# A hybrid SSD and delta-rule layer: TensorE's instructions kept in the order of the text, one gate moved to an earlier scan, scan steps put in another order

## The chip, the cores and the metric

The kernel runs on one core of one Trainium2 chip. The metric is device time in microseconds (us): the median of the kernel before is 2363.67 us over 3 runs (2360.88 to 2366.65). Engines are called PE (TensorE matmuls; PEld is its weight loads), DVE (VectorE), ACT (ScalarE), POOL (GpSimd) and SP (SyncE, which issues the DMAs).

## The reference

One transformer-like layer over 320 kept tokens (a prompt with meta tokens ahead of it, and a batch of one sampled stretch), model width 2048, everything in float32. Cut to what matters:

```python
u = _rmsnorm(x, norm_mix_w)
z_a, xbc_a, dt_a, qkv_b, z_b, beta_b, a_b, gate_a, gate_b = split(u @ w_in)
xbc, conv_a_new = _causal_conv(xbc_a, conv_a, ssd_conv_w, ssd_conv_b)   # then silu; xs, bm, cm
ya, ssm_a_new = _ssd_scan(xs, softplus(dt_a + bias), -exp(ssd_a_log), bm, cm, h0)  # 4 groups of 8 heads
ya = _rmsnorm((ya + xs * ssd_d) * silu(z_a), ssd_norm_w)
qkv, conv_b_new = _causal_conv(qkv_b, conv_b, gdn_conv_w)               # then silu, l2norm of q and k
# in _gdn_scan, for each block of tokens, 4 groups of 4 heads:
lmat = where(strict, beta * (k @ k.T) * decay, 0)
tinv = triangular_solve(eye + lmat, eye)
u = tinv @ (v * beta); w = tinv @ (k * beta * exp(gcum)); wv = u - w @ s
o = (q * exp(gcum)) @ s + (q @ k.T * decay) @ wv
ob = _rmsnorm(ob, gdn_norm_w) * silu(z_b)
h = x + sigmoid(gate_a) * (ya @ w_out[:2048]) + sigmoid(gate_b) * (ob @ w_out[2048:])
h = h + square(relu(_rmsnorm(h, norm_mlp_w) @ w_up)) @ w_down
```

The result is `_rmsnorm(h, norm_f_w)` and the new convolution and scan states.

## The kernel before

**The big products.** Every product with a weight is made by `block()` as matmuls into `pbig`. A chunk of weights of 512 x 256 comes by a DMA of SP into `raw` (`wload`, L195, three buffers), ACT rounds it to `hi` (L61), DVE makes the rest `lo` (L64), three buffers each, and PE multiplies three times for each of eight (j, k): hi by the high part of the tokens, hi by their low part, lo by the high part. So a chunk is 24 `pbig` matmuls of 320 to 336 columns. The chunks stand in one list, `stream`, in the order of use, and `block` loads three ahead. In the start `uh` and `ul` are the two parts of the normed tokens, made piece by piece (16 pieces) from `ut`; in the output projections `yh` and `yl` take their place.

**Main and side.** `run(main, side)` writes two generators in turn: `main` yields after three matmuls of `pbig` what they should take (3 x 325 / 2400 = 0.41 us for 320 columns), `side` yields what main work should pass before its next step. Beside the scan of one group stand the output projection of the group before and the projections of the group after. Four SSD scans (`scan_ssd`) come first, then four delta-rule scans (`scan_gdn`, here scan 0 to 3), then the MLP. Beside scan 0 stand `out_a(3)` and the projection for scan 1; beside scan 1 the first merge gate `gate_a`, `out_b(0)` and the projection for scan 2. The delta-rule projection has convolutions, `c` on DVE; `gate_a` has products `sgt`.

**What sets the order.** After the text is written, a scheduler puts the instructions of every engine in an order of its own, within the dependencies; the first stretch (up to `manual.close()`) already keeps the text's order. So in this kernel the yields propose an order and the scheduler decides it, on PE also.

**The start.** Rows `prow`, `cra`, `sra`, `crb`, `srb` are loaded and turned into columns by PE (`pcol`, L84), DVE copies them to `cwa`, `sta`, `cwb`, `stb`. `dvec` (L485) is loaded by pieces of 4 bytes, then four small `pb` (L487 to L490), then `wt` (L500, L501). ACT makes `nega` from `pb` and `wtr` from `wt`, and PE multiplies it into `ptok`. In `tokens()` that becomes `la`, and PE its running sums `pcum`.

**The SSD scan.** For each of three blocks of tokens PE makes `pcb` and the turned `pxt`; ACT and DVE make `xw` and its two parts `xwr`, which PE needs for the states `ph`; `em` and `xt` are needed for `pyd`, the sum of squares `sq` for `prs`.

**The delta-rule scan.** For each of three blocks PE makes `pk`, `pkk`, `pqk` and `pq` (the last one turns q); `a` goes to memory and comes back as blocks of 32 x 32 in `ab`. Then DVE alone solves all blocks, 31 steps of a product `pr` and a sum `ubt` (L847, L848). ACT copies the result to `ub`, DMAs write it (`uD`, `uTD`) and read it back as `u` and `tr` (L860, L866). Then come two rounds (32, then 64): PE `pz<-tr,a`, ACT `z<-pz`, in the first round PE `ptr<-z,u`, and PE `pu<-u,z`. For each block of tokens follow `pv`, `pw`, `po`, `pS`, and on DVE the norm `so`, `on`, which PE turns in `pot`. The yields between `pq` and `pz` are

```python
yield 1.0                      # after the last pq
yield 4.8                      # after the loads of ab
yield 0.5 + 0.0028 * w * m     # after each of the 31 steps
yield 9.6                      # after the loads of u and tr
```

where `w * m` sums to 7512 over the 31 steps, so the 31 yields are 36.5 us together and all of them 51.9 us.

Of the kernel before, what the change touches and what calls it, by code (L numbers as in the profile page):

```python
# [8 lines left out]
F32 = mybir.dt.float32  # L9
F32R = mybir.dt.float32r  # L10
AF = mybir.ActivationFunctionType
ALU = mybir.AluOpType
AX = mybir.AxisListType

P = 128
# [27 lines left out]
def tile_hybrid_step(ctx: ExitStack, tc: tile.TileContext, i: dict, o: dict):  # L43
# [16 lines left out]
    def act(out, in_, func=AF.Copy, **kw):  # L60
        nc.scalar.activation(out=out, in_=in_, func=func, **kw)  # L61
# [6 lines left out]

    V, G = nc.vector, nc.gpsimd
    MUL, ADD, SUB = ALU.mult, ALU.add, ALU.subtract  # L70


    ident = const.tile([P, P], F32, name="ident")
# [71 lines left out]
    def plan_proj(c0):  # L145
        plan([(0, win[:, c0:c0 + 256])], KD)

    def plan_out(r0):
        for b in range(8):
            plan([(0, wout[r0:r0 + 512, b * 256:(b + 1) * 256])], 4)  # L150
# [8 lines left out]
    def plan_gdn(g):  # L159
        for c0 in (C_K, C_Q, C_V, C_ZB):  # L160
            for b in range(2):
                plan_proj(c0 + g * 512 + b * 256)
# [7 lines left out]
    plan_out(1024)  # L170
    plan_gdn(0)
    plan_out(1536)
    plan_gdn(1)
    for b in range(8):
        plan_proj(C_GA + b * 256)
    plan_out(2048)
    plan_gdn(2)
    plan_out(2560)
# [334 lines left out]
    def tokens():  # L513

        yield 1.0
        for c in range(3):
            lo, n = CH_LO[c], CH_N[c]
            ps = scr("ptk")
            transp(ps[:n, :P], tokT[:, lo:lo + n])
            V.tensor_copy(tok[:n, c, :], ps[:n, :64])  # L520
            tt(V, tok[:n, c, :], tok[:n, c, :], ps[:n, 64:P], ADD)


        nega = sp.tile([P, 48], F32, name="nega")
        act(nega, pb[:, 1, :], AF.Exp)
        V.tensor_scalar(out=nega, in0=nega, scalar1=-1.0, scalar2=None, op0=MUL)
        sx = sp.tile([P, 3, 48], F32, name="sx")
        for a, b, t0 in ((0, 32, 0), (32, 48, 48)):
            tt(V, sx[:, :, a:b], tok[:, :, t0:t0 + b - a], pb[:, 0:1, a:b].to_broadcast([P, 3, b - a]), ADD)
        e = sp.tile([P, 3, 48], F32, name="e")  # L530
        s_ = sp.tile([P, 3, 48], F32, name="s_")
        s2 = sp.tile([P, 3, 48], F32, name="s2")
        pl = sp.tile([P, 3, 48], F32, name="pl")
        stt(e, sx, -1.0, sx, MUL, ALU.max)
        act(e, e, AF.Exp, scale=-1.0)
        V.tensor_scalar(out=s_, in0=e, scalar1=2.0, scalar2=None, op0=ADD)
        V.reciprocal(s_, s_)
        tt(V, s_, s_, e, MUL)
        tt(V, s2, s_, s_, MUL)
        V.tensor_scalar(out=pl, in0=s2, scalar1=1.0 / 17, scalar2=None, op0=MUL)  # L540
        for d in (15, 13, 11, 9, 7, 5, 3):
            stt(pl, pl, 1.0 / d, s2, ADD, MUL)
        stt(pl, pl, 1.0, s_, ADD, MUL)
        V.tensor_scalar(out=pl, in0=pl, scalar1=2.0, scalar2=None, op0=MUL)
        stt(pl, sx, 0.0, pl, ALU.max, ADD)
        V.tensor_copy(dt, pl[:, :, 0:32])
        la = sp.tile([P, 3, 48], F32, name="la")
        tt(V, la, pl, nega.unsqueeze(1).to_broadcast([P, 3, 48]), MUL)
        act(beta, tok[:, :, 32:48], AF.Exp, scale=-1.0)
        V.tensor_scalar(out=beta, in0=beta, scalar1=1.0, scalar2=None, op0=ADD)  # L550
        V.reciprocal(beta, beta)

        yield 13.5
        pcum = scr("pcum")
        ptot = scr("ptot")
        pv = pcum[:, :144].rearrange("p (c h) -> p c h", h=48)
        tv = ptot[:, :288].rearrange("p (c h) -> p c h", h=48)
        mm(pv[:80, 0, :], tri[:80, :80], la[:80, 0, :])
        mm(pv[:, 1, :], tri, la[:, 1, :])
        mm(pv[:, 2, :], trib, la[:, 2, :])  # L560
        mm(tv[:, 0, :], ones[:80, :], la[:80, 0, :])
        mm(tv[:, 1, :], ones, la[:, 1, :])
        mm(tv[:, 2, :], blk, la[:, 2, :])
        mm(tv[:, 3, :], halfm[:, 0, :], la[:, 2, :])
        mm(tv[:, 4, :], halfm[:, 1, :], la[:, 2, :])
        V.tensor_copy(acs[:80, 0, :], pv[:80, 0, :])
        V.tensor_copy(acs[:, 1:3, :], pv[:, 1:3, :])
        tt(V, wdec, tv[:, 0:3, :], acs, SUB)
        act(wdec, wdec, AF.Exp)
        act(etot[:, 0, :], tv[:, 1, :], AF.Exp)  # L570
        act(etot[:, 1:3, :], tv[:, 3:5, :], AF.Exp)
        act(neg_eg, acs[:, :, 32:48], AF.Exp)
        V.tensor_scalar(out=neg_eg, in0=neg_eg, scalar1=-1.0, scalar2=None, op0=MUL)
        tt(V, wd, dt, wdec[:, :, 0:32], MUL)
        yield 2.5
        rows = sp.tile([48, 2, NT], F32, name="rows")
        prow_ = scr("prow")
        for c in range(3):
            lo, n = CH_LO[c], CH_N[c]
            transp(prow_[:48, lo:lo + n], acs[:n, c, :])  # L580
        V.tensor_copy(rows[:, 0, :], prow_[:48, :NT])
        act(rows[:, 1, :], prow_[:48, :NT], AF.Exp)
        nc.scalar.dma_start(rowd.rearrange("a h t -> h a t"), rows)

        yield 1.0
# [19 lines left out]
    def scan_ssd(g, sg, x4, bc, z4):  # L605
# [12 lines left out]
        sti = sg.tile([P, 4, P], F32, tag="sio", name="sio", bufs=2)  # L618
        nc.sync.dma_start(sti, i["state_ssd"][0, 0, gh].rearrange("(t h) p n -> (h p) t n", h=2))
        load_decay(0)  # L620
        yield 4.0
        ps = scr("psi")
        for t in range(4):
            transp(ps[:, t * P:(t + 1) * P], sti[:, t, :])
# [6 lines left out]
        for c in range(3):  # L631
# [1 line left out]
            if c < 2:  # L633
                load_decay(c + 1)
            em = ems[c]

            for h in range(8):
                V.tensor_scalar(out=em[:n, h, :nl], in0=em[:n, h, :nl], scalar1=acs[:n, c, g * 8 + h:g * 8 + h + 1], scalar2=0.0, op0=SUB, op1=ALU.min)
            act(em[:n, :, :nl], em[:n, :, :nl], AF.Exp)
            ps = scr("pcb")  # L640
            mm(ps[:n, :nl], bc[:, 0, lo:lo + n], bc[:, 1, l0:l0 + nl])
            transp(ps[:n, 256:384], bc[:, 0, lo:lo + n])
            cb = sg.tile([P, P], F32, tag="cb", name="cb", bufs=2)
            tt(V, cb[:n, :nl], ps[:n, :nl], (trib if c == 2 else tri)[:n, l0 - lo:l0 - lo + nl], MUL)
            bt = [sg.tile([P, P], F32R, tag=f"bt{m}", name="bt", bufs=2) for m in range(2)]
            act(bt[0][:n], ps[:n, 256:384])
            tt(V, bt[1][:n], ps[:n, 256:384], bt[0][:n].bitcast(F32), SUB)
            for a in (0, 4):
                tt(G, em[:n, a:a + 4, :nl], em[:n, a:a + 4, :nl], cb[:n, None, :nl].to_broadcast([n, 4, nl]), MUL)

            ps = scr("pxt")
            for t in range(4):
                transp(ps[:n, t * P:(t + 1) * P], x4[:, t, lo:lo + n])
            xt = sg.tile([P, 512], F32, tag="xt", name="xt", bufs=1)
            xw = sg.tile([P, 512], F32, tag="xw", name="xw", bufs=1)
            psv, dtv = by_head(ps, n, dt[:n, c, gh])
            tt(V, xt[:n].rearrange("s (h p) -> s h p", p=64), psv, dtv, MUL)
            psv, wdv = by_head(ps, n, wd[:n, c, gh])
            tt(V, xw[:n].rearrange("s (h p) -> s h p", p=64), psv, wdv, MUL)
            xwr = [sg.tile([P, 512], F32R, tag=f"xw{m}", name="xwr", bufs=1) for m in range(2)]  # L660
# [1 line left out]
            tt(V, xwr[1][:n], xw[:n], xwr[0][:n].bitcast(F32), SUB)  # L662
            yz = sg.tile([P, 4, P], F32, tag="yz", name="yz", bufs=2)
            tt(G, yz[:, :, :nl], x4[:, :, l0:l0 + nl], dvec[:, g * 4:(g + 1) * 4].unsqueeze(2).to_broadcast([P, 4, nl]), MUL)
            yield 4.7 if c else 2.7

            new = []
            upd = [[(None, None, 0, n)], [(0, hp, 0, 128)], [(1, hp, 0, 64), (2, hs, 64, 128)]][c]
# [4 lines left out]
            for ph, (e, h, r0, r1) in zip(phs, upd):  # L673
                hn = sg.tile([P, 512], F32, tag="h", name="hn", bufs=4)
                if h is None:
                    act(hn, ph)
                else:
                    hv, ev = by_head(h, P, etot[:, e, gh])
                    tt(G, hn.rearrange("s (h p) -> s h p", p=64), hv, ev, MUL)
                    tt(V, hn, hn, ph, ADD)  # L680
                new.append(hn)
                yield 1.5
            if c:
                po = scr("pyo")
                pov = po.rearrange("p (t l) -> p t l", l=nl)
# [48 lines left out]
    def scan_gdn(g, sg, q4, k4, v4, z4):  # L734
# [164 lines left out]
        for c in range(3):  # L899
# [44 lines left out]
            for h in heads:  # L944
                for pS, (e, s, r0, r1) in zip(pSs, upd):
                    mm(pS[:, h, :], kw[c][r0:r1, h, :], wv[r0:r1, h, :])
            for pS, (e, s, r0, r1) in zip(pSs, upd):
                if s is None:
                    spr = t2k("S", "spr", 3)
                    act(spr, pS)  # L950
                else:
                    for h in heads:
                        stt(s[:, h, :], s[:, h, :], etot[:, e, 32 + g * 4 + h:33 + g * 4 + h], pS[:, h, :], MUL, ADD)
            if c == 2:
                nc.sync.dma_start(o["gdn_p"][0, 0, g * 4:(g + 1) * 4].rearrange("h k v -> k h v"), spr)
                nc.sync.dma_start(o["gdn_s"][0, 0, g * 4:(g + 1) * 4].rearrange("h k v -> k h v"), ss)

            so = small("so")
            ssq(po[:nx], nx, so)
            stt(so[:nx], so[:nx], 1.0 / P, qq[c][:nx], MUL, ADD)  # L960
            tt(G, so[:nx], so[:nx], nhalf_pow[:nx], ALU.pow)
            on = t2k("Ak", "on", 1)
            tt(V, on[:nx], po[:nx], b4(so, nx), MUL)
            yield 6.0
            yh, yl = ys[4 + g] = ys.get(4 + g) or new_y()
            pot = pview("pot")
            for h in heads:
# [85 lines left out]
        run(chain(out_a(2), kept(proj_gdn(0), tiles)), scan_ssd(3, sg, *tiles[3]))  # L1053
    with ExitStack() as sctx:
        sg = sctx.enter_context(tc.tile_pool(name="sgg", bufs=1))
        run(chain(out_a(3), kept(proj_gdn(1), tiles)), scan_gdn(0, sg, *tiles[4]))
        run(chain(gate_a(), out_b(0), kept(proj_gdn(2), tiles)), scan_gdn(1, sg, *tiles[5]))
        run(chain(out_b(1), kept(proj_gdn(3), tiles)), scan_gdn(2, sg, *tiles[6]))
        run(chain(out_b(2), gate_b()), scan_gdn(3, sg, *tiles[7]))

# [181 lines left out]
```

## Time and profile before

| | |
|---|---|
| median of 3 runs | 2363.67 us (2360.88 to 2366.65) |
| profiled execution: its own time | 2363.06 us |
| profiled execution: span of the trace | 2361.4 us |
| PE busy | 2312.0 us, 98% |
| DVE, ACT, POOL busy | 57%, 45%, 14% |
| chain that ended last | PE 93%, DVE 3%, DMA 1%, ACT 1% |

The span is what the trace covers; the execution's own time is 1.7 us longer. In a row of a timeline stand the start, the duration, engine and line, the operation, `out<-in`, how many, and in brackets the idle time just before it with what ended it. In a row of windows stand the stretch, its length, then for each engine its busy time and in brackets how many instructions began there, then the granted TensorE clock (1.00 is 2.4 GHz, 0.50 is 1.2 GHz).

### The profile page before, as it was taken

How to read it: one execution, taken by the hardware profiler on the slowest of the kernel's cores; microseconds unless marked ns; L12 is line 12 of the kernel's file. 1: busy time of each engine (PE TensorE's matmuls, PEld its weight loads, DVE VectorE, ACT ScalarE, POOL GpSimd, SP SyncE). 2: the span in 40 equal slices, each digit the busy share in tenths (PEclk: the TensorE clock that was granted, in tenths of full speed). 3: DMA queues.
4: the chain of work that ended last, by engine and by line, in shares of the span. 5: the costliest groups of instructions: out<-in, count | busy, mean ns of one | idle time of the engine just before them, and what ended most of it. 6: DMA issues, size and time to landing. Idle time of an engine off the chain costs nothing.

```text
span 2361.4 us, 40717 instructions
## 1 busy us (share of the span) xinstructions
PE 2312.0 (98%) x16393; PEld 2287.6 (97%) x16393; DVE 1348.4 (57%) x2147; ACT 1057.2 (45%) x1816; POOL 320.7 (14%) x488
## 2 busy tenths in 40 slices
PE   7999999999999999999999999999999999999997
PEld 6999999999999999999999999999999999999997
DVE  6675757665766764558657658444444444444443
ACT  5655545354455444544554435433343234324433
POOL 3142414141221210112212110000000000000000
PEclk8999999999999999999999999999999999999999
DMA  7746555555555665554545644544554454445543
GB/s 187 218 127 176 140 157 158 148 146 157 143 143 140 181 186 161 143 156 133 151 145 151 171 147 147 151 150 152 152 150 149 149 152 152 150 146 151 169 143 116
DMA packets 411558, 362.87 MB, mean 154 GB/s; under 512 B 48841, under 2 KB 408346, under 8 KB 410906
## 3 DMA queue, kind: packets, MB, share of 16 engines
q1 hardware_dynamic: 411258, 360.15, 52.2%
q8 instruction: 128, 2.10, 0.4%
q14 instruction: 60, 0.49, 0.1%
q10 hardware_dynamic: 112, 0.13, 0.0%
HBM read 340.57 MB, written 19.66 MB: 153 GB/s over the span
## 4 chain that ended last, share of the span: by engine, by line
PE 93%; DVE 3%; DMA 1%; ACT 1%; issue 0%; SPq 0%; POOL 0%; ACTq 0%; DVEq 0%
PE pbig L58 86%; PE po L58 1%; DVE lo L64 1%; DVE c L67 1%; PE pw L58 0%; PE pu L58 0%; PE ph L58 0%; PE pS L58 0%; PE pkk L58 0%; PE pqk L58 0%; PE pyd L58 0%; PE pz L58 0%; DMA x<-in_x_sample_dram 0%; PE pks L58 0%; DVE yl L64 0%
## 5 line engine op out<-in xcount | busy, mean ns | idle before, releaser
L64 DVE TENSOR_TENSOR lo<-raw,hi 128x1024 fp32r<-128x1024 f32 x591 | 735.9, 1246 | 674.7 <-ACT hi L61 673.4
L61 ACT ACTIVATE hi<-raw 128x1024 fp32r<-128x1024 f32 x592 | 626.2, 1058 | 898.9 <-PE pbig L58 823.7
L58 PE MATMUL pbig<-uh,hi 128*128 128x320 f32 (+2 forms) x2176 | 688.2, 316 | 0.0
L58 PE MATMUL pbig<-uh,lo 128*128 128x320 f32 (+2 forms) x2176 | 683.0, 314 | 3.9 <-DVE lo L64 3.9
L58 PE MATMUL pbig<-ul,hi 128*128 128x320 f32 (+2 forms) x2176 | 684.0, 314 | 2.3 <-DVE ul L67 2.3
L58 PEld LDWEIGHTS pbig<-uh,lo 128*128 128x128 f32 x2176 | 411.9, 189 | 5.7 <-DVE lo L64 4.7
L58 PEld LDWEIGHTS pbig<-uh,hi 128*128 128x128 f32 x2176 | 412.5, 190 | 4.3 <-issue 3.0
L58 PEld LDWEIGHTS pbig<-ul,hi 128*128 128x128 f32 x2176 | 412.4, 190 | 4.2 <-DVE ul L67 3.2
L58 PE MATMUL pbig<-hh,hi 128*128 128x320 f32 x1024 | 318.0, 311 | 0.0
L58 PE MATMUL pbig<-hnl,hi 128*128 128x320 f32 x1024 | 317.1, 310 | 0.0
L58 PE MATMUL pbig<-hl,hi 128*128 128x320 f32 x1024 | 316.2, 309 | 0.0
L58 PE MATMUL pbig<-hh,lo 128*128 128x320 f32 x1024 | 316.2, 309 | 0.0
L58 PE MATMUL pbig<-hnh,lo 128*128 128x320 f32 x1024 | 315.8, 308 | 0.0
L58 PE MATMUL pbig<-hnh,hi 128*128 128x320 f32 x1024 | 315.1, 308 | 0.0
L58 PEld LDWEIGHTS pbig<-hnh,lo 128*128 128x128 f32 x1024 | 192.9, 188 | 0.0
L58 PEld LDWEIGHTS pbig<-hl,hi 128*128 128x128 f32 x1024 | 192.6, 188 | 0.0
L58 PEld LDWEIGHTS pbig<-hh,hi 128*128 128x128 f32 x1024 | 192.6, 188 | 0.0
L58 PEld LDWEIGHTS pbig<-hnh,hi 128*128 128x128 f32 x1024 | 192.3, 188 | 0.2
L58 PEld LDWEIGHTS pbig<-hh,lo 128*128 128x128 f32 x1024 | 192.5, 188 | 0.0
L58 PEld LDWEIGHTS pbig<-hnl,hi 128*128 128x128 f32 x1024 | 192.2, 188 | 0.0
L58 PE MATMUL pbig<-yh,hi 128*128 128x320 f32 x512 | 160.9, 314 | 0.0
L58 PE MATMUL pbig<-yl,hi 128*128 128x320 f32 x512 | 157.5, 308 | 0.0
(303 smaller groups left out, 2411.8 us busy)
## 6 DMA issues: line engine op xcount, KB each, us to landing
raw<-in_w_in_dram SPq DMA_DIRECT2D x256, 512.0 KB, 3.9
raw<-in_w_up_dram SPq DMA_DIRECT2D x128, 512.0 KB, 3.8
raw<-in_w_down_dram SPq DMA_DIRECT2D x128, 512.0 KB, 3.4
raw<-in_w_out_dram SPq DMA_DIRECT2D x64, 512.0 KB, 3.5
raw<-in_w_in_dram SPq DMA_DIRECT2D x32, 256.0 KB, 3.4
em<-rowd SPq DMA_DIRECT2D x8, 512.0 KB, 6.2
u<-uD SPq DMA_DIRECT2D x12, 256.0 KB, 3.3
eab<-rowd SPq DMA_DIRECT2D x8, 336.0 KB, 5.6
```

Of the source, the lines that this page charges most:

```text
L58: nc.tensor.matmul(out, lhsT=lhsT, rhs=rhs, start=start, stop=stop, **kw)
L61: nc.scalar.activation(out=out, in_=in_, func=func, **kw)
L64: eng.tensor_tensor(out=out, in0=a, in1=b, op=op)
L67: nc.vector.scalar_tensor_tensor(out=out, in0=a, scalar=s, in1=b, op0=op0, op1=op1)
```

## The change

There are three parts. First, `tc.manual_schedule` holds PE, for the whole kernel, to the order in which the text writes its instructions; the other engines are still put in order by the scheduler. Second, `gate_a()` moves from beside delta-rule scan 1 to beside scan 0, between `out_a(3)` and the projection for scan 1; the list of weight chunks moves with it. Third, steps and yields of the scans: in `scan_ssd` the products `pcb` and `pxt` and what makes `xwr` stand first, and `cb`, `xt` and `em` after them, the yields are 3.6 and 4.4 instead of 4.7 (2.7 for the first block) and 1.5, and 14.0 instead of 4.0 ahead of `psi` in groups 1 to 3; in `scan_gdn` the norm `so` is begun before the update of the state, with 6.6 instead of 6.0 ahead of `pot`; in `tokens()` 15.5 instead of 13.5 stands ahead of `pcum`. The yields between `pq` and `pz` are as they were.

```diff
     MUL, ADD, SUB = ALU.mult, ALU.add, ALU.subtract
+    ctx.enter_context(tc.manual_schedule(engines={mybir.EngineType.PE}))
...
     plan_out(1536)
-    plan_gdn(1)
     for b in range(8):
         plan_proj(C_GA + b * 256)
+    plan_gdn(1)
     plan_out(2048)
...
-        yield 13.5
+        yield 15.5
         pcum = scr("pcum")
...
-        yield 4.0
+        yield 14.0 if g else 4.0
         ps = scr("psi")
...
-            for h in range(8):
-                V.tensor_scalar(out=em[:n, h, :nl], in0=em[:n, h, :nl], scalar1=acs[:n, c, g * 8 + h:g * 8 + h + 1], scalar2=0.0, op0=SUB, op1=ALU.min)
-            act(em[:n, :, :nl], em[:n, :, :nl], AF.Exp)
             ps = scr("pcb")
...
-            cb = sg.tile([P, P], F32, tag="cb", name="cb", bufs=2)
-            tt(V, cb[:n, :nl], ps[:n, :nl], (trib if c == 2 else tri)[:n, l0 - lo:l0 - lo + nl], MUL)
...
-            for a in (0, 4):
-                tt(G, em[:n, a:a + 4, :nl], em[:n, a:a + 4, :nl], cb[:n, None, :nl].to_broadcast([n, 4, nl]), MUL)
-            ps = scr("pxt")
+            pcb, ps = ps, scr("pxt")
...
-            psv, dtv = by_head(ps, n, dt[:n, c, gh])
-            tt(V, xt[:n].rearrange("s (h p) -> s h p", p=64), psv, dtv, MUL)
             psv, wdv = by_head(ps, n, wd[:n, c, gh])
...
-            yield 4.7 if c else 2.7
+            cb = sg.tile([P, P], F32, tag="cb", name="cb", bufs=2)
+            tt(V, cb[:n, :nl], pcb[:n, :nl], (trib if c == 2 else tri)[:n, l0 - lo:l0 - lo + nl], MUL)
+            psv, dtv = by_head(ps, n, dt[:n, c, gh])
+            tt(V, xt[:n].rearrange("s (h p) -> s h p", p=64), psv, dtv, MUL)
+            for h in range(8):
+                V.tensor_scalar(out=em[:n, h, :nl], in0=em[:n, h, :nl], scalar1=acs[:n, c, g * 8 + h:g * 8 + h + 1], scalar2=0.0, op0=SUB, op1=ALU.min)
+            act(em[:n, :, :nl], em[:n, :, :nl], AF.Exp)
+            for a in (0, 4):
+                tt(G, em[:n, a:a + 4, :nl], em[:n, a:a + 4, :nl], cb[:n, None, :nl].to_broadcast([n, 4, nl]), MUL)
+            yield 3.6
...
-                yield 1.5
+            yield 4.4
...
-            yield 6.0
+            yield 6.6
             yh, yl = ys[4 + g] = ys.get(4 + g) or new_y()
...
-        run(chain(out_a(3), kept(proj_gdn(1), tiles)), scan_gdn(0, sg, *tiles[4]))
-        run(chain(gate_a(), out_b(0), kept(proj_gdn(2), tiles)), scan_gdn(1, sg, *tiles[5]))
+        run(chain(out_a(3), gate_a(), kept(proj_gdn(1), tiles)), scan_gdn(0, sg, *tiles[4]))
+        run(chain(out_b(0), kept(proj_gdn(2), tiles)), scan_gdn(1, sg, *tiles[5]))
```

What this does to the order of PE is seen at three places. At the start, PE's row before, just behind `prx`:

```order
L58 MATMUL prx<-dgx,ones 128x112 x3
L84 MATMUL pcol<-ident,cra 128x96
L58 MATMUL pbig<-uh,hi 128x336
L58 MATMUL pbig<-uh,lo 128x336
L58 MATMUL pbig<-ul,hi 128x336
...
L84 MATMUL pcol<-ident,sra 128x72
```

The same place now; 93 `pbig` stand between `prx` and the first `pcol`:

```order
L58 MATMUL prx<-dgx,ones 128x112 x3
L58 MATMUL pbig<-uh,hi 128x336
...
L87 MATMUL pcol<-ident,cra 128x96
L87 MATMUL pcol<-ident,sra 128x72
L87 MATMUL pcol<-ident,crb_473 128x96
L87 MATMUL pcol<-ident,srb_479 128x72
L87 MATMUL pcol<-ident,crb_474 128x96
L87 MATMUL pcol<-ident,srb_480 128x72
L58 MATMUL ptok<-uh,wtr 128x336
```

The turn of `cra`, which stood ahead of the first `pbig`, stands with the other five behind the 93 `pbig`.

In an SSD scan, from `pxt` to the states `ph`, before:

```order
L84 MATMUL pxt<-ident,x_298 128x128 x4
...
L58 MATMUL pbig<-uh,lo 128x336
L58 MATMUL ph<-xwr,bt 128x512
L58 MATMUL pbig<-uh,hi 128x336
L58 MATMUL pbig<-ul,hi 128x336
L58 MATMUL ph<-xwr,bt 128x512 x2
```

And now:

```order
L87 MATMUL pxt<-ident,x_300 128x128 x4
...
L58 MATMUL pbig<-uh,hi 128x336
L58 MATMUL pbig<-ul,hi 128x336
L58 MATMUL pbig<-uh,lo 128x336
L58 MATMUL ph<-xwr,bt 128x512 x3
```

The products of `ph` stand together, behind 24 to 33 `pbig` counted from `pxt`.

In delta-rule scan 0, where `pz` and what follows it stand, before (`tr` and `u` come by DMA from the solve, `z` from ACT):

```order
L58 MATMUL pz<-tr,a 32x32 x5
L58 MATMUL pbig<-uh,lo 128x324
L58 MATMUL pbig<-uh,hi 128x324
L58 MATMUL pbig<-ul,hi 128x324
...
L58 MATMUL pz<-tr,a 32x32 x15
L58 MATMUL ptr<-z,u 32x32 x8
L58 MATMUL pu<-u,z 32x32 x20
L58 MATMUL pz<-tr,a 64x64 x8
```

And now:

```order
L58 MATMUL pz<-tr,a 32x32 x20
L58 MATMUL pbig<-uh,hi 128x320
L58 MATMUL pbig<-ul,hi 128x320
L58 MATMUL pbig<-uh,lo 128x320
...
L58 MATMUL ptr<-z,u 32x32 x8
L58 MATMUL pu<-u,z 32x32 x20
...
L58 MATMUL pz<-tr,a 64x64 x8
```

Twelve `pbig` now stand between `pz` and `ptr`, where none stood. Between the last `pq` and the first `pz` of scans 0 to 3 there are 408, 396, 396 and 408 `pbig` now; before there were 485, 450, 485 and 485.

## Rows read from the trace of the kernel before

**Rows 1.** Page, its first lines: span, and PE's busy time, share and instructions

```profile
span 2361.4 us, 40717 instructions
...
PE 2312.0 (98%) x16393; PEld 2287.6 (97%) x16393; DVE 1348.4 (57%) x2147; ACT 1057.2 (45%) x1816; POOL 320.7 (14%) x488
```

**Rows 2.** Waits of PE, whole run: us in total, times, longest

```profile
PE pcol L84 <- DMA cra<-in_ssd_conv_w_dram: 8.1, 1, 8.1
PE ph L58 <- ACT xwr L61: 4.7, 4, 1.4
PE ptr L58 <- ACT z L61: 4.3, 4, 1.6
PE pbig L58 <- DVE lo L64: 3.9, 3, 1.3
PE pot L84 <- DVE on L64: 2.8, 3, 1.1
...
PE ph L58 <- DVE xwr L64: 1.8, 2, 1.2
PE pcum L58 <- DVE la L64: 1.7, 1, 1.7
```

**Rows 3.** Windows: delta-rule scans 0 to 3, from the last pq to pz

```profile
614.30:688.40 74.10, 72.82 (x485) 72.37 (x484) 57.77 (x109) 32.64 (x61) 20.13 (x27) 1.00 0.60 158
793.10:859.00 65.90, 65.90 (x452) 65.70 (x450) 50.46 (x91) 25.66 (x37) 15.37 (x16) 1.00 0.73 207
1082.60:1156.70 74.10, 72.81 (x485) 72.39 (x484) 57.77 (x109) 32.61 (x61) 19.79 (x27) 1.00 0.58 159
1262.60:1335.00 72.40, 71.08 (x486) 70.67 (x484) 54.53 (x98) 26.31 (x36) 14.46 (x13) 1.00 0.65 180
```

**Rows 4.** Timeline of DVE: before and at the first solve step, and the last sums

```profile
798.73 0.14 DVE L64 TENSOR_TENSOR pr<-ubt,ab 112x1 f32<-112x1 f32 x1
...
1094.50 0.49 DVE L64 TENSOR_TENSOR acc<-acc,pbig 128x320 f32<-128x320 f32 x1 [1.27 <-PE pbig L58]
1094.91 0.15 DVE L64 TENSOR_TENSOR pr<-ubt,ab 112x1 f32<-112x1 f32 x1
...
1140.81 0.69 DVE L848 TENSOR_REDUCE ubt<-pr 112x16 f32<-112x512 f32 x1
...
1319.00 0.68 DVE L848 TENSOR_REDUCE ubt<-pr 112x16 f32<-112x512 f32 x1
```

**Rows 5.** DVE by group, the solve of scan 2 (1094.9 to 1141.5): busy us, mean ns

```profile
L64 DVE TENSOR_TENSOR lo<-raw,hi 128x1024 fp32r<-128x1024 f32 x14 | 17.0, 1218 | 0.0
L64 DVE TENSOR_TENSOR pr<-ubt,ab 112x1 f32<-112x1 f32 (+30 forms) x31 | 12.7, 410 | 0.7
...
L67 DVE SCALAR_TENSOR_TENSOR c<-pre,cwb,c 128x339 f32<-128x339 f32 x12 | 6.8, 566 | 0.0
```

**Rows 6.** SP's timeline, last loads of tr in scan 2; landing times of tr

```profile
1148.24 1.12 SPq L866 DMA_DIRECT2D tr<-uTD x2
...
DMA to landing us min/median/max: 3.7/3.7/3.8
```

**Rows 7.** Windows at a low clock: at the start, in scans 0, 1 and 2

```profile
26.90:33.60 6.70, 6.49 (x23) 6.00 (x24) 6.30 (x10) 3.03 (x5) 2.98 (x2) 0.50 0.12 25
...
692.40:702.70 10.30, 10.30 (x98) 9.54 (x96) 5.54 (x7) 5.72 (x11) 1.15 (x2) 0.50 0.43 111
863.00:869.90 6.90, 6.90 (x36) 6.36 (x37) 2.98 (x3) 3.71 (x7) 0.96 (x1) 0.51 0.45 119
1160.00:1170.30 10.30, 10.04 (x103) 9.31 (x104) 6.22 (x8) 6.30 (x13) 1.15 (x2) 0.50 0.35 97
```

**Rows 8.** Timelines of PE and ACT at the start

```profile
26.87 0.39 PE L84 MATMUL pcol<-ident,cra 96*128 96x96 f32 x1 [8.11 <-DMA cra<-in_ssd_conv_w_dram]
...
42.08 0.24 ACT L61 ACTIVATE nega<-pb 128x48 f32<-128x48 f32 x1 [4.12 <-DMA pb<-in_gdn_a_log_dram]
...
47.37 1.15 ACT L61 ACTIVATE wtr<-wt 128x512 fp32r<-128x512 f32 x2 [3.10 <-DMA wt<-in_w_in_dram]
```

More of the change, by code (lines that the diff above doesn't have):

```diff
@@ L946, in scan_gdn, with update @@
                     mm(pS[:, h, :], kw[c][r0:r1, h, :], wv[r0:r1, h, :])
[L947 to L953, printed above, removed]
+            def update(pS, e, s):
+                for h in heads:
+                    stt(s[:, h, :], s[:, h, :], etot[:, e, 32 + g * 4 + h:33 + g * 4 + h], pS[:, h, :], MUL, ADD)
+            so = small("so")
+            ssq(po[:nx], nx, so)
+            if c == 0:
+                spr = t2k("S", "spr", 3)
+                act(spr, pSs[0])
+            else:
+                update(pSs[0], *upd[0][:2])
+            stt(so[:nx], so[:nx], 1.0 / P, qq[c][:nx], MUL, ADD)
+            tt(G, so[:nx], so[:nx], nhalf_pow[:nx], ALU.pow)
+            if c == 2:
+                update(pSs[1], *upd[1][:2])
+            on = t2k("Ak", "on", 1)
+            tt(V, on[:nx], po[:nx], b4(so, nx), MUL)
             if c == 2:
@@ L956, in scan_gdn @@
                 nc.sync.dma_start(o["gdn_s"][0, 0, g * 4:(g + 1) * 4].rearrange("h k v -> k h v"), ss)
[L958 to L963, printed above, removed]
-            yield 6.0
+            yield 6.6
             yh, yl = ys[4 + g] = ys.get(4 + g) or new_y()
```

## The prediction

> **What bounds the kernel.** I read the head of the page first: PE is busy for 2312.0 of 2361.4 us [rows 1]. The change keeps the number of `pbig` matmuls, so it can only move PE's idle time (49.4 us by the page) and the time that PE spends at the low clock. The waits of PE come next: what they name is what an order can take away [rows 2]. Last come the places where the new order makes PE ask for something earlier than before. These do not show as waits before; they are found as slack, from the time at which the data were ready and the time at which PE wanted them [rows 3 to 6]. Here that is the way from the last `pq` to the first `pz`, once in each of four delta-rule scans.
>
> **The solve: why I expect new waits.** In scan 2 PE ran 485 `pbig` from the last `pq` to `pz` in 74.1 us and did not wait at `pz`; without its one wait of 1.3 us (the longest of the three for `lo` [rows 2]) that is 72.8 / 485 = 0.150 us for each [rows 3]. In the text there are only 396. The yields ask for 51.9 us there, 36.5 of them for the 31 steps, while DVE took from 1094.91 to 1140.81 + 0.69 = 1141.50, so 46.6 us, for these steps [rows 4]: besides `pr` (12.7 us) and as many `ubt` it does 17.0 us of `lo` and 6.8 us of `c` [rows 5], and it is full. So the text puts `pz` too early, and the scheduler had moved it back by 89 `pbig`. PE held to the text no longer can.
>
> The chain of data in scan 2, from the end of the last `pq` at 1082.6: 12.3 us to the first step (DVE has sums `acc` ahead of it that wait for PE [rows 4]; they stand in the same order in both kernels), 46.6 for the steps, then ACT's copy and the DMAs. The last `tr` is issued at about 1148.8 (the second of two from 1148.24) and lands 3.7 us later [rows 6], at 1152.5, 11.0 us behind the steps. Together 69.9 us. PE's new way is 396 x 0.150 + 1.3 = 60.7 us. It waits 9.2 us at `pz`, bounds 8 and 10.3 (a chain 1.2 us, one `lo`, shorter, or PE without its wait).
>
> - Scan 0: now beside `gate_a`. The 12 `c` (6.8 us) go, four `sgt` come, which I price as the sum of equal shape, 0.49 us each [rows 4], so 2.0, and one `lo` fewer (1.2) stands in the steps: 46.6 - 6.0 = 40.6 us if DVE alone sets the pace. Scan 3, which has no `c` either, took 1319.68 - 1274.9 = 44.8 us (its first step again 12.3 us behind 1262.6 [rows 3, 4]), since the `lo` also wait for PE's progress. I take 43. 12.3 + 43 + 11.5 = 66.8, against 408 x 0.150 + 1.3 = 62.5: wait 4.3 (1.8 to 7.0).
> - Scan 1: the first step comes 798.73 - 793.1 = 5.6 us behind the last `pq` [rows 3, 4]; one more `lo` now stands ahead of it (1.2), and the steps now carry the convolutions, as in scan 2: 6.8 + 46.6 + 11.0 = 64.4, against 396 x 0.1464 (65.9 / 450 [rows 3]) to 0.150, so 58.0 to 59.4: wait 5.5 (2 to 7).
> - Scan 3: 12.3 + 43 (one `lo` fewer than its 44.8) + 12.4 (its loads were issued more slowly; an estimate, 1.4 above scan 2) = 67.7, against 408 x 0.147 (71.1 / 485 [rows 3]) + 1.3 = 61.3: wait 6.4 (4.9 to 8.7).
>
> The sum is 25.4 us, bounds 16.7 to 33.0. Behind a waiting `pz` stand all later `pbig` in PE's row, which is the whole price. The rows show no other work that could fill it.
>
> **What the change takes away.** Each of these waits has its own row [rows 2].
> - `ptr <- z`, 4.3 us: twelve `pbig` (1.8 us) now stand between `pz` and `ptr`, more than the longest wait (1.6). All goes: -4.3 (0 to -4.3).
> - `pot <- on`, 2.8 us: the norm is begun before the state's update, and the yield is longer by 0.6. All goes: -2.8 (0 to -2.8).
> - `ph <- xwr`, 4.7 + 1.8 = 6.5 us: `xwr` now stands at the head of DVE's and ACT's work, with 24 to 33 `pbig` behind `pxt`. I take two thirds: -4.5 (0 to -6.5). What is late next is `pyd`, which needs `em` and `xt`; 33 `pbig` (5 us) stand ahead of it, and I count it at nothing (0 to +3).
> - `pcum <- la`, 1.7 us: 111 `pbig` instead of 122 stand ahead of it, while `la` is made by the same DVE steps. I take -0.8 (0 to -1.7), and -0.5 for the clock behind it.
> - `pbig <- lo`, 3.9 us: DVE's order in the solve is nearly the same, so they stay: 0 (0 to -3.9).
>
> **The start.** `pcol` waited 8.1 us for `cra` and held the first `pbig` to 26.97 us [rows 8]. In the text `pcol` comes behind 93 `pbig`, so the wait goes and `pbig` starts about 6 us sooner. But ACT's `nega`, which waits for `pb` until 42.08, still stands ahead of the last four pieces `uh` (its order has not changed there), and `wt` lands at 47.3 [rows 8]. Both are DMAs queued behind `dvec`, and no earlier `pbig` makes them land sooner. So PE gets to the twelfth piece about 6 us sooner and waits there for about 7 us. The `ptok` behind needs `wtr` as before, and two `pcol` now need a PSUM buffer that DVE frees behind its `wtr`. I take +1.4 us (-1 to +4); if the 6 us are kept after all, -6.
>
> **The clock.** In scans 0 to 2 the granted clock was 0.5 for 10.3, 6.9 and 10.3 us [rows 7], each time just behind the waits and the small matmuls at `pz`, `ptr` and `pu`; at half the speed that cost about 13.7 us. The `ptr` waits go, but the four new ones are longer: the wait of 8.1 us at the start was followed by 6.7 us at 0.5 [rows 7, 8]. If each costs 3.4 us (half of 6.8, the middle row), that is 13.6 again: 0. If each costs half of 10.3, +6.9; if only two do, -6.9. The Trainium skill, TensorE: Matmul & The Clock Gate, section "HAM oscillation — how this bites in real kernels", tells of a kernel in which every tile waits for its DMA and so every tile begins at the low clock; it speaks against this change, since four places with short waits become four waits for a DMA. The low rows here agree in kind. By that rule all four stalls would drop the clock, and with the long row's length the sum would be 2384 instead of 2377.
>
> **The rest** (projections, MLP, stores) keeps its order: 0.
>
> **Sum.** +25.4 +1.4 -0.8 -0.5 -4.5 -4.3 -2.8 +0 = +13.9. The profiled execution's own time was 2363.06, which is 0.6 under the median of the runs shown, so 2377.0; I do not correct the 0.6. **Forecast: 2377 us**, its own range 2366 to 2390.
>
> **Rivals.**
> 1. *Faster: the data come sooner.* If the `acc` sums ahead of the first step no longer wait, scans 0, 2 and 3 start their steps as early as scan 1 did, 5.6 instead of 12.3 us behind the last `pq`. Then the waits are 0, 5.5, 2.5 and 0 us, 8 instead of 25.4, and two stalls fewer spare 6.9 us of clock: 2377 - 17.4 - 6.9 = 2353. For it: PE runs the same `pbig` in any case, and scan 1 shows that it can be so. Against it: DVE's order has the same sums ahead of the first step, each waits for PE, and PE's pace is the same.
> 2. *Faster: the wait costs nothing, since PE goes on with the `pbig` behind `pz`.* Then only the gains are left: -0.8 - 0.5 - 4.5 - 4.3 - 2.8 + 1.4 and up to -13.7 of clock, 2338 to 2352. Against it: at `ptr` PE stood idle for 1.6 us with `pbig` behind it in its row. The Trainium skill, same page, section "The mechanism", says that matmuls start and end in program order and only weight loads are pulled ahead; this trace agrees, with the 4.3 us of `ptr`.
> 3. *No change.* The waits come out at the lower bounds (16.7), and the start keeps its 6 us: 2377 - 8.7 - 7.4 = 2361, or with only the first of them and the clock spared once (3.4) 2365.
> 4. *Slower by more.* All solve waits at the upper bounds and the clock at +6.9: 2377 + 7.6 + 6.9 = 2391.
> The point from which it decides: the gains are 12.9 us less the 1.4 of the start, so the change breaks even where the four waits sum to 11.5 us.
>
> **How the numbers follow.** A measurement of this kernel can tell about 0.2% (4.7 us) from no change. The forecast and rival 4, both slower, have 0.68: all bounds of the waits but the very lowest leave it over 2368.4. Rival 3, between 2359 and 2368, has 0.15. Rivals 1 and 2 together have 0.17, nearly all of it rival 1 or a mixture with a gain at the start. The range goes from 2355, inside rival 1, to 2390, short of rival 4's end.
>
> **What would show it.** Right: before the first `pz` of each delta-rule scan PE idles 4 to 10 us, ended by a DMA of `tr` or `u`; waits at `ptr` and `pot` are gone, those at `ph` nearly; the wait for `cra` is gone, but PE waits some 7 us in the start for `uh` or `ul`, with `nega` still waiting for `pb`, and `ptok` begins near 50 us; the clock is low behind each stall. Wrong: `pz` without a wait, a first step less than 10 us behind the last `pq` in scans 0, 2 and 3, or a DVE that ends its 31 steps in clearly less than 43 us.

## The result and the profile of the changed kernel

The changed kernel takes 2376.86 us (median of 4 runs, 2375.02 to 2378.46) against 2364.01 us for the kernel before in the same comparison (4 runs): a ratio of 1.0052, 95% interval 1.0039 to 1.0064. It is slower by about 12.9 us. The forecast was 2377 us. In two of the experiments below one execution of four took several times as long as the others, and the time given is the median of the other three.

PE's waits in the changed kernel come first: what waited, for what, us in total, times, the longest. Compare [rows 2].

```profile
PE pz L58 <- DMA tr<-uTD: 24.3, 8, 7.4
PE pbig L58 <- DVE lo L64: 6.3, 5, 1.6
PE pbig L58 <- ACT uh L61: 4.2, 2, 2.3
PE pbig L58 <- DVE ul L67: 3.9, 4, 2.1
PE prs L58 <- POOL sq L64: 3.7, 4, 1.6
...
PE pcol L87 <- DVE cwa L309: 1.2, 1, 1.2
...
PE ph L58 <- DVE xwr L64: 0.2, 1, 0.2
```

The waits at `pcol` for `cra`, at `ptr`, at `pot` and at `pcum` are gone and `ph` has 0.2 us left of 6.5, so the order of PE and the reordered scan steps do what they were meant to. In their place stands one entry that was not there: `pz`, 24.3 us for a DMA of `tr`. Smaller are the new wait for `uh` (4.2), more at `prs` (3.7 instead of 0.6), and more for `lo` and `ul`.

PE's timeline shows the first `pz` of each of the four delta-rule scans (the second row of each scan, the next `pz` that had to wait for another part of `tr`, is shown for scan 0 alone):

```profile
672.66 0.47 PE L58 MATMUL pz<-tr,a 32*32 32x32 f32 x10 [3.44 <-DMA tr<-uTD]
674.21 1.01 PE L58 MATMUL pz<-tr,a 32*32 32x32 f32 x30 [1.08 <-DMA tr<-uTD]
...
968.50 0.73 PE L58 MATMUL pz<-tr,a 32*32 32x32 f32 x10 [7.45 <-DMA tr<-uTD]
...
1152.19 0.74 PE L58 MATMUL pz<-tr,a 32*32 32x32 f32 x10 [7.11 <-DMA tr<-uTD]
...
1333.60 0.74 PE L58 MATMUL pz<-tr,a 32*32 32x32 f32 x10 [3.26 <-DMA tr<-uTD]
```

The windows from the last `pq` to the first `pz`, to be read against [rows 3] (length; busy time and instructions of PE, PEld, DVE, ACT, POOL; granted clock):

```profile
607.60:672.60 65.00, 59.99 (x408) 59.47 (x406) 52.49 (x96) 24.83 (x34) 14.14 (x12) 1.00 0.61 171
899.50:968.50 69.00, 60.10 (x397) 59.30 (x395) 53.67 (x99) 33.83 (x66) 21.88 (x25) 0.97 0.55 148
1083.40:1152.20 68.80, 60.08 (x397) 59.30 (x395) 56.86 (x108) 30.62 (x57) 17.71 (x25) 0.97 0.55 149
1268.70:1333.60 64.90, 60.02 (x409) 59.50 (x407) 52.68 (x96) 24.79 (x34) 15.14 (x13) 1.00 0.61 168
```

PE is busy for 60.0 to 60.1 us in each, while the windows last 65 to 69 us; the difference is idle time, ahead of `pz` and, for about 1.6 us in each, at `lo`. Before, 450 to 485 `pbig` covered the same chain.

Where the 12.3 us between the two traces (spans 2373.7 and 2361.4 us) arise can be followed by one `pq` after another. The window of the last `pq` of scan 0 begins at 607.6 instead of 614.3, so 6.7 us ahead; that of scan 2 at 1083.4 instead of 1082.6, 0.8 behind; that of scan 3 at 1268.7 instead of 1262.6, 6.1 behind [rows 3]; the end is 12.3 behind. The change wins 6.7 us up to the first delta-rule scan, and then loses 19 us in the four of them (behind them, the last 6000 `pbig` begin 899.5 us ahead of the end in both traces).

### The profile page after: what moved, and what is told of

It reads as the page before. It is cut to its first block, busy times and chain, and to the rows that moved or that the text cites. A ratio compares the mean times of both kernels' runs of the same rounds, so it can differ in the third digit from the quotient of the medians.

```text
span 2373.7 us, 40688 instructions
## 1 busy us (share of the span) xinstructions
PE 2308.9 (97%) x16393; PEld 2284.7 (96%) x16393; DVE 1356.8 (57%) x2147; ACT 1060.3 (45%) x1822; POOL 345.9 (15%) x488
## 4 chain that ended last, share of the span: by engine, by line
PE 85%; DVE 9%; DMA 2%; issue 1%; ACT 1%; POOL 1%; SPq 0%; ACTq 0%; DVEq 0%; POOLq 0%
PE pbig L58 78%; DVE lo L64 3%; DVE ubt L851 2%; DVE pr L64 1%; DVE c L67 1%; PE po L58 1%; DMA raw<-in_w_in_dram 1%; DMA tr<-uTD 1%; POOL yz L64 1%; PE pS L58 0%; PE pw L58 0%; ACT hi L61 0%; PE pkk L58 0%; PE pqk L58 0%; DVE ul L67 0%
```

## The experiments

The theory: PE, held to the text, comes to `pz` before the solve's data do, and nothing behind `pz` may run; the loss is the difference of two times, 396 to 408 `pbig` on PE and a chain of DVE, ACT and DMAs. Rivals: the moved gate costs, the reordered scan steps make the solve late, or the waits are only a sign of a solve that PE itself slows, so that a later `pz` would move them.

**pz later.** On the changed kernel:

```diff
-        yield 9.6
+        yield 18.6
```

> The changed kernel with 18.6 instead of 9.6 in the yield ahead of the first pz of each delta-rule scan, so 66 more pbig stand between the last pq and pz (462 to 474, near the 450 to 485 of the kernel before). Theory (the four waits at pz, 24.3 us in the trace of the changed kernel, are the loss): pz finds its data, the waits go to under 2 us in all, and the low clock behind them (about 12 us of PE's time in that trace) goes too or stays: 2340 if it goes, 2352 if it stays. Rival (the solve is only late because PE held back the lo that DVE makes between its steps, so a later pz only moves the wait): pz still waits 4 us or more, time over 2365.

Measured: 2349.82 us, ratio to the kernel before 0.9951 (0.9934 to 0.9967). No wait at `pz` is left in this run. Two entries of its list of waits, and its two rows of PE ahead of `pz` in scan 0:

```profile
PE pbig L58 <- DVE lo L64: 7.9, 7, 1.6
...
PE pbig L58 <- ACT hi L61: 1.7, 2, 1.4
```

```profile
678.23 0.41 PE L58 MATMUL pbig<-uh,hi 128*128 128x320 f32 x1 [1.37 <-ACT hi L61]
...
679.49 0.41 PE L58 MATMUL pbig<-uh,lo 128*128 128x320 f32 x1 [0.70 <-DVE lo L64]
...
680.71 1.49 PE L58 MATMUL pz<-tr,a 32*32 32x32 f32 x40
```

One number in the text turns a kernel that is 0.5% slower than before into one that is 0.5% faster. The rival of a solve slowed by a PE that waits falls: with `pz` later the 31 steps take 43.3, 51.4, 46.5 and 43.3 us in the four scans, where they took 43.3, 51.2, 46.7 and 43.2. Of the two times expected it is the upper one: in scan 0 a new wait for `hi` and `lo` stands just ahead of `pz` (1.37 + 0.70 us), and the clock is low behind it, in this window of that run at 0.57 on the mean:

```profile
680.00:692.00 12.00, 12.00 (x141) 11.11 (x140) 5.54 (x7) 5.20 (x8) 1.12 (x2) 0.57 0.62 192
```

**The same with half the shift.** `yield 14.1` instead of 9.6.

> The changed kernel with 14.1 instead of 9.6 in the yield ahead of the first pz, so 33 more pbig (4.9 us) instead of the 66 of the run with 18.6. Theory (PE and the chain of the solve run side by side, the wait is their difference): the waits of 4.5, 8.1, 7.6 and 4.0 us at pz become 0, 3.2, 2.7 and 0, together about 6 us; time 2356, between 2352 and 2361. Rival (a wait costs by its number and its low clock, not by its length): scans 1 and 2 cost as much as before, 2362 or more.

Measured: 2353.88 us (ratio 0.996, 0.9947 to 0.9972). Its waits at `pz`:

```profile
PE pz L58 <- DMA tr<-uTD: 7.2, 6, 2.0
```

The waits are 7.2 us where 6 were expected, and the time lies in the range (the trace is of the longest of nine runs, 2349.89 to 2358.16 us). By scan they are 0.7, 3.1, 3.1 and 0.3 us, where 0, 3.2, 2.7 and 0 were expected: the 33 `pbig` more, 4.9 us of work, took 5.1 and 4.5 us off the waits in scans 1 and 2, and nearly all of the shorter waits in scans 0 and 3. Half the shift already gives most of the gain, 23.0 of 27.0 us; one reason is that it does not have the `hi` wait of the full shift.

**The gate alone.** The kernel before, with only the first merge gate beside scan 0:

```diff
-    plan_gdn(1)
     for b in range(8):
         plan_proj(C_GA + b * 256)
+    plan_gdn(1)
...
-        run(chain(out_a(3), kept(proj_gdn(1), tiles)), scan_gdn(0, sg, *tiles[4]))
-        run(chain(gate_a(), out_b(0), kept(proj_gdn(2), tiles)), scan_gdn(1, sg, *tiles[5]))
+        run(chain(out_a(3), gate_a(), kept(proj_gdn(1), tiles)), scan_gdn(0, sg, *tiles[4]))
+        run(chain(out_b(0), kept(proj_gdn(2), tiles)), scan_gdn(1, sg, *tiles[5]))
```

> The kernel before with only the gate moved beside scan 0 (PE still in the scheduler's order). Theory: the scheduler puts 485 to 489 pbig ahead of pz in all four scans, so no wait at pz, and the ptr, pot and ph waits stay: 2364, within 4. Rival (the place of the gate is what costs): 2370 or more.

Measured: 2366.3 us, ratio 1.0025 (1.0015 to 1.0036), no wait at `pz`. The time lies within the 4 us that were allowed around 2364. The rise is small but clear of no change: 4.5 us against the 2361.77 us of the kernel before on that chip, which is more than expected and less than the rival's. Its place is `ptr`:

```profile
PE ptr L58 <- ACT z L61: 5.9, 4, 3.2
...
PE pu L58 <- ACT z L61: 0.7, 1, 0.7
```

Scan 1 now stands beside the convolutions, and on ACT the copy `z` that `ptr` waits for comes behind `pre`, `c` and `q` of these. The two rows are 2.3 us more than the 4.3 of [rows 2], and `lo` (5.4 us here) adds 1.5, while `pot` gives back 1.1: together the 2.7 to 2.8 us by which this trace's span (2364.2 us) is longer. So in this trace the gate's place costs a little where the scheduler puts `pz` and `ptr` side by side. PE in the text's order has twelve `pbig` there, and the wait at `ptr` is gone in the changed kernel. The other combination, PE in the text's order with the gate left beside scan 1, was not tried.

**Without PE's order.** The changed kernel without the line:

```diff
-    ctx.enter_context(tc.manual_schedule(engines={mybir.EngineType.PE}))
```

> The changed kernel without the line that holds PE to the order of the text; gate and scan steps as changed. Theory: the scheduler moves pz back behind 485 to 489 pbig, no wait at pz; the waits at pot and ph shrink by 2 to 7 us, ptr and the wait for cra stay: 2359, between 2355 and 2364. Rival (the scan steps themselves make the solve late): waits at pz, 2370 or more.

Measured: 2364.32 us, ratio 1.0008 (0.9999 to 1.0017): no difference from the kernel before can be told. No wait at `pz`, so the rival (the scan steps make the solve late) falls; but the time lies just over the upper end of what was expected (2364). The waits at `pot` are gone and 0.2 us is left at `ph`; `ptr` has the 5.9 + 0.7 us of the run before, and the clock is low behind it in all four scans where it was low in three. The window of scan 1:

```profile
980.00:992.00 12.00, 12.00 (x85) 11.12 (x80) 5.92 (x7) 4.82 (x9) 0.96 (x1) 0.57 0.46 133
```

The order of PE by itself, on top of the other two parts, is 2376.86 - 2364.32 = 12.5 us, nearly the whole loss. (The two were compared on different occasions, with 2364.01 and 2361.77 us for the kernel before; by the ratios it is 0.44%, 10.4 us.) In this trace 485 to 489 `pbig` stand between the last `pq` and `pz`, in that of the changed kernel 396 to 408.

**Without the reordered scan steps.** PE in the order of the text and the gate moved, the scans and yields as before:

> PE in the order of the text and the gate moved, but the scan steps and yields as in the kernel before. Theory: the waits at pz are as in the changed kernel (24 us), ptr without a wait; ph waits as before or more, pot waits again since its norm comes later: 2382, between 2377 and 2388. Rival (the reordered steps delay the solve): the waits at pz shrink to under 15 us, time under 2372.

Measured: 2394.29 us, ratio 1.014 (1.0125 to 1.0155). This is more than the expected range. The waits at `pz` are as expected, and the miss is at `ph`:

```profile
PE pz L58 <- DMA tr<-uTD: 23.6, 8, 6.7
PE ph L58 <- ACT xwr L61: 8.1, 4, 2.5
...
PE ph L58 <- DVE xwr L64: 6.1, 5, 2.9
```

I had counted `ph` as before or a little more (6.5 us); it is 14.2. Some 5 of the 7.7 us more stand in the third block of groups 1 to 3, where the scheduler had put 40 `pbig` between `pxt` and `ph` and the text has 33, so there it had moved `ph` back too. Most of the rest stands in the second block of group 0, where the count is 33 in both and DVE's `xwr` comes later. The waits at `pot`, which I had expected back, did not come back. Behind the waits at `ph` the clock is low in the SSD scans, at 0.57 from 148 to 156 us for one. So the reordered steps are worth 17 us (2394.29 - 2376.86; by the ratios 21) as soon as PE keeps the text's order. Without it they are worth at most about 2 us (2366.3 - 2364.32), and the two intervals touch. The same cause as at `pz` costs at `ph` wherever the text puts it ahead of its data.

**The start.** I had said that the 6 us by which `pbig` starts sooner are given back, because `pb` and `wt` stand in SP's queue behind the loads of `dvec`. On the kernel with 18.6:

```diff
-    for h in range(2):
-        nc.sync.dma_start(dvec[h * 64:(h + 1) * 64, :], i["ssd_d"][0].rearrange("(t h) -> h t", h=2)[h].partition_broadcast(64))
...
     nc.sync.dma_start(wt[:, :, 32:64], win[:, C_BETA:C_BETA + 32].rearrange("(k p) c -> p k c", p=P))
+    dv = sp.tile([P, 32], F32, name="dv")
+    nc.sync.dma_start(dv, i["ssd_d"][0].partition_broadcast(P))
...
+        for h in range(2):
+            b = slice(h * 64, (h + 1) * 64)
+            V.tensor_copy(dvec[b], dv[b].rearrange("p (t h) -> p h t", h=2)[:, h])
```

> The kernel with 18.6 ahead of pz, and ssd_d loaded behind wt as 128 rows of 32 numbers, from which DVE copies dvec later, in place of two loads in pieces of 4 bytes. Theory (the start is bound by pb and wt, whose DMAs stand behind those of dvec): pb lands before 37 us instead of 42, wt before 43 instead of 47, ptok starts near 43 instead of 48.3 us, and the time falls by 4 to 6 us against the run with 18.6: 2345. Rival (the start is bound by the pieces uh and ul that ACT and DVE make): ptok still near 48, time as with 18.6, 2350.

Measured: 2344.41 us, ratio 0.9922 (0.9906 to 0.9939), 5.4 us under the run with 18.6. ACT in the changed kernel first, then ACT in this run:

```profile
40.85 0.24 ACT L61 ACTIVATE nega<-pb 128x48 f32<-128x48 f32 x1 [7.83 <-DMA pb<-in_gdn_a_log_dram]
...
46.23 1.15 ACT L61 ACTIVATE wtr<-wt 128x512 fp32r<-128x512 f32 x2 [3.27 <-DMA wt<-in_w_in_dram]
```

```profile
29.91 0.23 ACT L61 ACTIVATE nega<-pb 128x48 f32<-128x48 f32 x1
...
38.43 1.17 ACT L61 ACTIVATE wtr<-wt 128x512 fp32r<-128x512 f32 x2
```

In the changed kernel ACT stood still for 7.8 us for `pb` (7.7 in the run with 18.6); here neither `nega` nor `wtr` waits for a DMA. `ptok` starts at 42.77 us in this run, against 48.26 in the run with 18.6:

```profile
42.77 0.40 PE L58 MATMUL ptok<-uh,wtr 128*128 128x336 f32 x1
```

The theory holds. With the loads of `dvec` no longer ahead of `pb` and `wt`, the early start is kept to the end of the kernel. The edit changes both the place of these loads and their pieces, so it does not tell which of the two counts.

**prs later.** On the kernel with 18.6, 8.6 instead of 7.0 ahead of `prs`:

> The kernel with 18.6 ahead of pz, and in the SSD scans 8.6 instead of 7.0 in the yield ahead of prs (12 more pbig). Theory: the wait of prs for POOL's sq (3.7 us in four) goes, and nothing else becomes late: 2346, 3 to 4 us under the run with 18.6. Rival (the later prs makes yh and yl late, or the low clock eats it): 2349 to 2353.

Measured: 2351.03 us (ratio 0.9952, 0.9937 to 0.9967), so nothing gained: the rival. The waits at `prs` are gone, and two others stand at the first group of the SSD scans, where `prb` and then the output projection need what comes behind `prs`:

```profile
199.09 0.49 PE L58 MATMUL prb<-dg,ones 128*128 128x128 f32 x2 [1.38 <-DVE dg L602]
...
202.83 0.64 PE L58 MATMUL pbig<-yh,hi 128*128 128x320 f32 x1 [2.38 <-ACT yh L61]
```

**Both.** The rows of `ssd_d` and 8.6 together:

> Both edits on top of 18.6: ssd_d in rows, and 8.6 ahead of prs. Theory: the two gains lie in different stretches and add up, 2341, between 2338 and 2345. Rival (either gain is given back in a later wait): 2346 or more.

Measured: 2347.36 us (ratio 0.9935, 0.9919 to 0.9952), so 3.0 us more than with `ssd_d` alone: the rival. The wait at `yh` is there again with 2.4 us, and moving `prs` gains nothing on either kernel.

**pz later only as far as needed.** On the kernel with `ssd_d` in rows:

```diff
-        yield 18.6
+        yield 18.6 if g in (1, 2) else 15.0
```

> The kernel with ssd_d in rows, with 18.6 ahead of pz only in scans 1 and 2 and 15.0 in scans 0 and 3 (447 instead of 474 pbig). In scan 0 of the run with 18.6 everywhere, PE waited 2.3 us for hi and 0.7 for lo some 3 us ahead of pz, since the loads of raw stood on SP behind the loads of u and tr, and the clock was low for 6.8 us behind it. Theory (that wait is the time in which the small matmuls at pz could stand): with pz ahead of that place the wait shrinks to 1 us or less and the low clock with it: 2341, between 2338 and 2343. Rival (the place does not matter, the loads of raw land when they land): hi still waits 2 us, 2344.

Measured: 2337.69 us, ratio 0.9894 (0.9875 to 0.9914), just under the lower end of what was expected (2338). This is the fastest version, about 25 us under the kernel before. The wait for `hi` is gone, `pz` waits nowhere, and the clock is full around it in all four scans. From the last `pq` of scan 0 to that of scan 1 this trace has 286.9 us, the one with 18.6 everywhere 292.0. Scans 0 and 1 of this run:

```profile
660.00:700.00 40.00, 39.31 (x373) 37.95 (x372) 18.91 (x27) 19.78 (x39) 7.69 (x9) 1.00 0.69 201
950.00:990.00 40.00, 40.00 (x374) 38.93 (x373) 23.32 (x36) 24.22 (x59) 8.62 (x21) 1.00 0.57 160
```

Why the 27 `pbig` less mattered is seen on ACT and SP in the run with `ssd_d` in rows and 18.6 everywhere:

```profile
673.81 1.06 ACT L61 ACTIVATE hi<-raw 128x1024 fp32r<-128x1024 f32 x1 [10.41 <-DMA raw<-in_w_in_dram]
```

```profile
662.91 2.03 SPq L866 DMA_DIRECT2D u<-uD x2
...
666.05 1.01 SPq L872 DMA_DIRECT2D tr<-uTD x2
...
668.15 1.81 SPq L198 DMA_DIRECT2D raw<-in_w_in_dram x3
```

The loads of weights stand on SP behind the loads of `u` and `tr`, which have to wait for the writes of the solve. PE runs out of chunks some 14 us after the last step of the solve (658.2 us in that run). In the last version the 40 small matmuls of `pz` are done by then and the work is spread otherwise; that the time of the small matmuls covers the late load is my reading of the two traces, and was not taken apart further.

## Why the prediction was right

- **What decides.** The step on which the forecast stood, 25.4 us of new waits at `pz`, measured 24.3. By scan 4.5, 8.1, 7.6 and 4.0 us (the first and second wait of each added), against 4.3, 5.5, 9.2 and 6.4. The sum is better than its parts: scan 0 is inside its bounds, scan 1 lies 1.1 over its upper one, scans 2 and 3 lie 0.4 and 0.9 under their lower ones.
- **Scan 1** was mis-sized because I priced its solve as that of scan 2, 46.6 us. It took 51 us (906.4 to 957.6), and 51 us too in the run with the gate alone, so the longer solve comes with the place of the gate and not with PE's order. PE's way was longer too, 61.6 us instead of 58.0 to 59.4, which took back some of it. DVE was not full there:

```profile
L64 DVE TENSOR_TENSOR lo<-raw,hi 128x1024 fp32r<-128x1024 f32 x14 | 17.1, 1219 | 7.0 <-ACT hi L61 6.9
L64 DVE TENSOR_TENSOR pr<-ubt,ab 112x1 f32<-112x1 f32 (+30 forms) x31 | 12.7, 409 | 0.8
```

  The columns are busy time, mean ns of one, and the idle time before them. Ahead of some `lo` DVE idles 7.0 us for `hi`, where [rows 5] have 0.0. Most of it is one place, two rows of ACT and one of DVE:

```profile
913.12 0.44 ACT L61 ACTIVATE acc<-pbig 128x320 f32<-128x320 f32 x1 [1.32 <-PE pbig L58]
913.46 1.05 ACT L61 ACTIVATE hi<-raw 128x1024 fp32r<-128x1024 f32 x1
...
914.54 1.23 DVE L64 TENSOR_TENSOR lo<-raw,hi 128x1024 fp32r<-128x1024 f32 x1 [4.93 <-ACT hi L61]
```

  Beside `out_b(0)` the sums are copies `acc` on ACT, and four of them, each waiting 1.3 us for PE, stand ahead of this `hi`. So the solve there follows PE's progress by way of ACT. That the `lo` between the steps follow PE I had used for scans 0 and 3, but not for scan 1.
- **Scans 2 and 3**: in scan 2 PE needed 61.7 us to `pz` (the window of 68.8 less the wait of 7.1), not 60.7, and in scan 3 the chain was 66.4 us (1268.7 to the landing just ahead of the second `pz` at 1335.1), not 67.7: the 12.4 us that I had put on its loads were 10.7. (By its own numbers, 69.9 - 59.4, the upper bound of scan 2 should read 10.5 and not 10.3.)
- **ptr and pot**: forecast -4.3 and -2.8, and both waits are gone. **ph**: forecast -4.5, measured -6.3. What came late in its place is `prs`, +3.1, which I had not named (I had named `pyd`).
- **lo**: forecast 0, measured +2.4 (6.3 instead of 3.9): two more short waits in scan 1 (1.5 us in all), and the three that were there are 0.3 us longer each.
- **pcum**: forecast -0.8 and -0.5 for the clock. The wait of 1.7 us is gone and so is the 3.4 us of low clock from 78 us on, which was worth half of that, so about -3.4. I had taken `la` to be made by the same steps of DVE. Those are the same, but the scheduler put one `lo` and three `c` fewer ahead of it, and it comes 4.0 us sooner (before, then changed):

```profile
76.23 0.30 DVE L64 TENSOR_TENSOR la<-pl,nega 128x144 f32<-128x144 f32 x1
```

```profile
72.21 0.30 DVE L64 TENSOR_TENSOR la<-pl,nega 128x144 f32<-128x144 f32 x1
```

- **The start**: forecast +1.4, measured -0.1 (`ptok` starts at 48.64 instead of 48.78 us). The mechanism was right and the experiment with `ssd_d` shows it: 5.5 us sooner at the first `pbig`, given back by a wait of 1.9 us for `uh`, 1.6 us more for `ul`, and a stretch at the low clock ahead of `ptok` (0.80 on the mean from 40.0 to 48.6 us).
- **The clock**: forecast 0. The low stretches in the delta-rule scans add up to about 34 us against 27 before, but some 10 us of them lie in the waits themselves, where they cost nothing; what is left of the balance when the other terms are taken off the 19 us is under 1 us. The four stretches were 3.4, 10.2, 13.7 and 6.8 us long, where I had put 6.8 for each, so the term came out right by other sizes. The clock was low behind all four stalls, as in this window of the changed kernel.

```profile
1148.00:1164.00 16.00, 11.36 (x136) 10.57 (x136) 3.58 (x7) 3.39 (x8) 1.63 (x5) 0.57 0.45 125
```

  The rule of the Trainium skill that I set beside it (TensorE: Matmul & The Clock Gate, section "HAM oscillation — how this bites in real kernels") is borne out in kind. Its sum, 2384, was too high, since two of the four stretches were short (3.4 and 6.8 us).

  One row I had misread. The 6.7 us at the low clock in the start [rows 7] do not show what a wait of 8.1 us does, since the clock was low before PE began to wait for `cra` (at 18.8 us):

```profile
16.60:26.90 10.30, 2.19 (x11) 1.72 (x10) 3.71 (x8) 5.69 (x11) 3.74 (x4) 0.50 0.48 130
```

- **The sum** by parts: start and `pcum` -3.7 (the first `psi` at 118.48 instead of 122.17 us; forecast +0.1), SSD scans -3.0 (-4.5), delta-rule scans +19.0 (+18.3), together +12.3 against +13.9. So errors of 0.7 to 3.8 us stand in it with both signs, and part of the close agreement is luck.
- **The rivals**: the first (the data come sooner) needed a first step less than 10 us behind the last `pq`; in scan 2 it was at 1095.7, 12.3 behind, as before. The second (PE goes on behind a waiting `pz`) is excluded by the waits. The point from which it decides was put at 11.5 us of waits. The run with half the shift has 7.2 us and is faster, the changed kernel has 24.3 us and is slower; so far the runs agree with it, without testing the point itself. The working names two lower ends of its range, 2366 and 2355; 2376.86 lies in both.

## What to carry to other kernels

An order written by hand is as good as the times written into it: where an in-order engine is taken away from a scheduler, look for each place where it had moved a consumer back, and compare the cover that the text gives (here 396 to 408 matmuls, some 61.7 us with waits of 1.6 for `lo`) with the measured length of the chain of the producers (66 to 70 us), transfers included. A consumer that has slack in the trace before shows no wait there; its slack has to be worked out from the landing of its data. The gain of such an order comes only as far as these places have their cover: the same change cost 0.5% and, with two numbers and one load altered, gained 1.1%.

## What the runs showed of the hardware

- Short waits behind which PE runs small matmuls can cost more by the clock than by themselves: with 18.6 everywhere the 2.1 us of waits in scan 0 were followed by a window of 12 us at 0.57, some 5 us of lost time by an estimate from these two figures. In the kernel before, a wait of 0.6 us at `ptr` in scan 1 stood ahead of 6.9 us at 0.51 [rows 7]. In the last version no stretch after the start, up to the last 10 us, is at the low clock.
- Two loads in pieces of 4 bytes, 64 x 16 numbers each, took 12.4 and 14.4 us to land in the changed kernel, and the small loads behind them on the same queue came late: with the same numbers loaded as 128 rows of 32, behind the others, ACT's `nega` ran at 29.9 instead of 40.9 us.
- Between runs of kernels that are alike in the start, PE's waits for the first loads of x add up to 3.5 to 6.2 us, so single profiles cannot tell differences of less than about 2.7 us there.
